# The entry into attention of a fused transformer layer: in what order the row maxima of the first two attention units are worked out

## The chip, the cores and the metric

The kernel runs on one core of a Trainium2 chip. It has five engines with a queue each: TensorE (PE in the profile, its weight loads PEld), VectorE (DVE), ScalarE (ACT), GpSimd (POOL) and SyncE (SP), which here only issues DMAs. The metric is the time of one execution in microseconds (us), as the median of several. Stretches and places below are in us from the start of the profiled execution's span.

## The reference, cut to what matters

One layer over 2048 latent tokens of width 1024, with 256 context tokens in front. What bears on the change is the gates at the end of the input projection, and the attention:

```python
p_x = h_x @ w_in[l]                      # ... q, u, vg, ga (gate_attn), gb (gate_gmlp)
k_all = jnp.concatenate([k_c, k_x], axis=2)      # 256 context + 2048 latent keys
v_all = jnp.concatenate([v_c, v_x], axis=2)
attn_x = merge_heads(attend_blocked(q_x, k_all, v_all))
...
def attend(q, k, v):
    s = jnp.einsum('bkgqd,bknd->bkgqn', q, k, preferred_element_type=jnp.float32)
    p = jax.nn.softmax(s, axis=-1).astype(v.dtype)
    return jnp.einsum('bkgqn,bknd->bkgqd', p, v)
```

There are 8 query heads of 64 columns and 2 key/value heads. A softmax needs a reference for each query, here its largest score, ahead of the exponentials.

## The kernel before

**Gates.** The projection ends with eight gate groups (`Gate`, g = 0 to 7) on a block of 1024 tokens. Each is computed with seven products in the place of eight (p in the order 0, 1, 5, 6, 4, 2, 3, the table `SUMS`), and each product is 12 matmuls of 128x512: four slices of 128 rows by three terms of a split number (lines 1742 to 1744). The last two groups, 6 and 7, run interleaved: (6,0), (7,0), (6,1), (7,1), (6,5), (7,5), and so on to (6,3), (7,3). Below, (g,p) is product p of group g. PSUM is eight banks of 128x512, in two groups of four while the projection runs (`psum({"a": 4, "b": 4})`). Group 6 holds one bank of "a" through all of its products, group 7 one of "b". Between products ScalarE moves seeds in and out of that bank and takes the tanh (line 2167), and VectorE adds sums (lines 2181 and 2186).

**Units.** Attention has 16 units (`Unit`): a block of 512 queries by two heads. `u` is the first unit and `v` the second. For each unit come, in this order:

- `load`, `cast`, `remainder`: its queries come from DRAM and are split into a high and a low half (casts on ScalarE, line 2217; remainders on VectorE, line 2223).
- `maxima(n)`: the next n of 18 items on a list. An item is a matmul for each of the two heads (four of half the width for the two context items), with 64 rows of the array each, head 0 in rows 0 to 63 and head 1 in rows 64 to 127 (line 2240), and behind them one reduction per head on VectorE over 512 columns (lines 2246 and 2251). Each item takes two banks.
- `reference`: one small reduction over all partial maxima (line 2258).
- `leading`: a transpose on PE (line 2266), a copy on ScalarE (line 2268) and eight small DMAs on SP (line 2271), which put the reference into the low half's first row.
- for each of 18 key tiles j, in three groups of six: `first` and `second`, two score matmuls each (lines 2285 and 2304; `second` reads the low half and so the reference), two exponentials on ScalarE (line 2308), later `values` (line 2316) and `gather`, the sum of the exponentials on GpSimd or VectorE (lines 2336 and 2333).

In `attend`, while unit i runs, the maxima of unit i + 1 are worked out, three at a time at two places of the first and second group. The first unit has no unit ahead of it. So the function `tail`, which the projection calls after each product of the last gates, does the first unit's maxima and the first six of the second unit's. Before: two of the first unit's behind each of nine products from (6,5) on; all that is left, `reference`, `leading` and six of the second unit's behind the last product, (7,3). Attention then opens all eight banks as one group.

**What sets the order.** The code emits instructions, and the tile framework's scheduler may reorder them on each engine, by what they wait for. Ranges in `self.fixed` keep PE and VectorE in the written order; the whole of `attend` is such a range, the end of the projection is not. Before, all maxima take banks of group "b", of which group 7 holds one: three are left for items that need two.

Of the kernel before, what the change touches and what calls it, by code (L numbers as in the profile page):

```python
# [29 lines left out]
TB = 512  # L30
# [20 lines left out]
def f32(ap):  # L51
    return ap.bitcast(F32)
# [20 lines left out]
class Kern:  # L73
# [1178 lines left out]
    def attend(self, units, late, mod):  # L1252
        self.psum({"b": 8})
        begin = self.here()
        old, pend = None, []

        def run(lo, hi):
            for j in pend[lo:hi]:
                owner.values(j)

        def ordered(work):
            at = self.here()
            work()
            self.loads.append(range(at, self.here()))

        def gather():
            for j in pend:
                owner.gather(j)

        for i, u in enumerate(units):  # L1270
            at = lambda n: units[n] if 0 <= n < len(units) else None
            nxt, far, old, older = at(i + 1), at(i + 2), at(i - 1), at(i - 2)
            for gi, g in enumerate(range(0, NKT, GROUP)):
                group = range(g, g + GROUP)
                step = nxt if gi < 2 else far
                for j in group:
                    u.first(j)
                    u.second(j)
                    if j % GROUP == 2 and far and gi == 0:
                        far.load()  # L1280
                    if j % GROUP == 4 and nxt and gi == 2:
                        ordered(nxt.leading)
                    if not nxt:
                        ordered(lambda: next(late, None))
                owner = u if gi else old
                run(0, 1)
                if step:
                    step.maxima(3)
                run(1, 4)
                if gi == 1 and far:  # L1290
                    far.cast()
                if gi == 2 and old:
                    old.sums()
                if step:
                    step.maxima(3)
                run(4, GROUP)
                if gi == 0:
                    if old:
                        old.leave()
                    u.o = self.bank([TB])  # L1300
                gather()
                if gi == 0:
                    if i:
                        next(mod, None)
                    if older:
                        older.inverse()
                if gi == 2 and far:
                    far.remainder()
                if gi == 1:
                    if nxt:  # L1310
                        nxt.reference()
                    if old:
                        old.join()
                pend = list(group)
        for _ in mod:
            pass
        owner = units[-1]
        for j in pend:
            owner.values(j)
            owner.gather(j)  # L1320
        units[-2].inverse()
        units[-1].join([self.sb("raw", [TB]) for _ in range(2)])
        self.fixed.append(range(begin, self.here()))
# [664 lines left out]
    def build(self):  # L1988
        self.constants()
        self.mod_head()  # L1990
        units = [Unit(self, b, p) for b in range(NB) for p in range(NH // 2)]
        self.KA, self.KB, self.V = ([None] * (NB + 1) for _ in range(3))
        for c in range(NB + 1):
            self.KA[c], self.KB[c] = [None] * NKV, [None] * NKV

        def key_load(kv):
            for c in range(NB + 1):
                n = TB if c else CTX
                ka = self.KA[c][kv] = self.h2([TB], F32R)
                self.nc.sync.dma_start(f32(ka[:, :n]), self.k_d[c][kv][:, :n])  # L2000

        def low_load(kv):
            for c in range(NB + 1):
                n = TB if c else CTX
                kb = self.KB[c][kv] = self.h2([TB], F32R)
                self.nc.sync.dma_start(f32(kb[HD:, :n]), self.k_d[c][kv][:HD, :n])
                self.nc.scalar.copy(kb[:HD, :n], self.lead[:HD].broadcast_to([HD, n]))

        def value_load(cs):
            for c in cs:  # L2010
                n = TT if c else CTX // P
                v = self.V[c] = self.h2([TT, P])
                src = self.rows(self.pr_d[0][c - 1][0], slice(P, 2 * P)) if c else self.vc_d[:, :n]
                self.nc.sync.dma_start(v[:, :n], src)

        def tail(g, p):
            u, v = units[0], units[1]
            n = KC - 2
            if (g, p) == (n + 1, 0):
                u.load()  # L2020
                key_load(0)
                u.cast()
                u.remainder()
            elif (g, p) == (n + 1, 1):
                low_load(0)
            elif (g, p) == (n, 5):
                u.maxima(2)
            elif g >= n and p not in (0, 1):
                if (g, p) == (n + 1, 5):
                    v.load()  # L2030
                    v.cast()
                    v.remainder()
                    value_load((0, 1))
                if (g, p) == (n + 1, 6):
                    key_load(1)
                    value_load((2, 3, 4))
                if (g, p) == (n + 1, 4):
                    low_load(1)
                u.maxima(2)
                if (g, p) == (n + 1, 3):  # L2040
                    u.maxima(len(u.todo))
                    u.reference()
                    u.leading()
                    v.maxima(6)

        self.project(tail)
        self.close("front")
        self.open("mid")
        self.open("pre", side="right")
        first = {}  # L2050
        late = self.br_inputs(0, first)
        self.g1b = self.sb("g1", [D])
        mod = self.mod_part(lambda: self.sb("raw", [TB]), ("g1",))
        self.attend(units, late, mod)
        h, w = self.operand_lists(), {0: {}}
        w1 = self.w1_ops(0, w[0], True)
        late = self.merge(first, late, units[-1], h, w1)
        self.ffn(h, w, w1, late)
        self.close("rest", "back", "pre")
        self.psum_stack.close()  # L2060
        self.order()
# [134 lines left out]
class Unit:  # L2196
# [28 lines left out]
    def maxima(self, n):  # L2225
        k, nc = self.k, self.nc
        for _ in range(n):
            if not self.todo:
                return
            c, t = self.todo.pop(0)  # L2230
            halves = ((0, slice(0, HD), k.KA), (1, slice(HD, P), k.KB))
            ps = [k.bank([TB]) for _ in range(2)]
            for s in range(2) if c == "ctx" else (0,):
                tok = slice((t + s) * P, (t + s + 1) * P)
                for h, rows, keys in halves:
                    if c == "ctx":
                        out, key = ps[h][:, s * CTX : (s + 1) * CTX], keys[0][self.kv]
                    else:
                        out, key = ps[h], keys[c][self.kv]
                    nc.tensor.matmul(  # L2240
                        out, self.qa[h][rows, tok], key[rows, : out.shape[-1]],
                        start=True, stop=True,
                    )
            for h in range(2):
                if c == "ctx":
                    nc.vector.tensor_reduce(
                        out=self.mx[:, t : t + 2, h, 0:1],
                        in_=ps[h].rearrange("p (s k) -> p s k", s=2), axis=AX.X, op=ALU.max,
                    )
                else:  # L2250
                    nc.vector.tensor_reduce(  # L2251
                        out=self.mx[:, t, h, c : c + 1], in_=ps[h], axis=AX.X, op=ALU.max
                    )
# [175 lines left out]
```

## Time and profile before

| | us |
|---|---|
| median of 3 runs (lowest, highest) | 3018.83 (3016.13, 3022.55) |
| profiled execution, its own time | 3009.05 |
| span of the profiled execution | 3007.2 |
| PE busy in the span | 2931.6 |
| DVE busy | 2062.5 |
| ACT busy | 1417.9 |
| POOL busy | 652.8 |
| maxima reductions on DVE (line 2251), 512 of them | 313.0 |
| mean granted TensorE clock | 0.994 |

The profile shows one execution. The clock is a share of full speed. The durations of PE's matmuls overlap, since a matmul starts before the one before it has ended, so how long one really takes is read from the distance of two starts. "Idle before" names, behind an arrow, what ended a wait.

### The profile page before, as it was taken

The page shows a single profiled execution, that of the slowest core. Times are in us where ns is not written, and L with a number is a line of the kernel's source. Part 1 is how long each engine was busy: PE and PEld are TensorE (multiplying, and loading weights), DVE is VectorE, ACT ScalarE, POOL GpSimd, SP SyncE. Part 2 cuts the span into 40 slices and gives each one's busy share as a digit, 9 for nine tenths or more (in the row PEclk, how much of TensorE's full clock was granted, in tenths as well). Part 3 has the DMA queues.
Part 4 walks back from the last instruction along what each step waited for, and adds up shares of the span by engine and source line. Part 5 has one row for each costly group of instructions (what it writes and reads, how often), then busy time and mean ns, then how long its engine had stood idle before and what let it go on. Part 6 is the DMA issues. An engine that isn't in the chain of part 4 may idle for free. (4 is left out here: it accounts for less than half of the span.)

```text
span 3007.2 us, 37935 instructions
## 1 busy us (share of the span) xinstructions
PE 2931.6 (97%) x13325; PEld 2206.7 (73%) x13325; DVE 2062.5 (69%) x2983; ACT 1417.9 (47%) x2318; POOL 652.8 (22%) x470
## 2 busy tenths in 40 slices
PE   7899999989999999999999989999999999999999
PEld 5778788876555555556888878888887888888887
DVE  5866487765788888867555587776676766654555
ACT  5554865553544545444222354444454344444432
POOL 0000000001999899894211200000000000000000
PEclk9999999999999999999999999999999999999999
DMA  7587866774010010016776658888766544447564
GB/s 276 184 295 272 307 215 217 256 247 140 24 36 26 25 37 22 22 36 191 238 215 194 183 198 308 307 305 303 261 219 224 186 154 154 154 154 277 210 209 155
DMA packets 386175, 559.04 MB, mean 186 GB/s; under 512 B 38640, under 2 KB 192416, under 8 KB 385984
## 3 DMA queue, kind: packets, MB, share of 16 engines
q1 hardware_dynamic: 373616, 535.89, 53.7%
q10 hardware_dynamic: 12368, 20.73, 1.8%
q8 instruction: 105, 1.72, 0.2%
q14 instruction: 86, 0.70, 0.1%
HBM read 379.75 MB, written 176.69 MB: 185 GB/s over the span
## 5 line engine op out<-in xcount | busy, mean ns | idle before, releaser
L2251 DVE TENSOR_REDUCE ts<-b 128x1 f32<-128x512 f32 x512 | 313.0, 681 | 75.3 <-PE b L2240 75.2
L2336 POOL TENSOR_TENSOR ac<-ac,p 128x512 f32<-128x512 f32 x214 | 306.3, 1463 | 50.5 <-ACT p L2308 50.5
L1858 DVE TENSOR_TENSOR b<-b,b 128x1024 fp32r<-128x1024 f32 x170 | 200.7, 1220 | 135.7 <-ACT b L1857 135.4
L1857 ACT CAST b<-b 128x1024 fp32r<-128x1024 f32 x170 | 170.6, 1050 | 222.2 <-PE b L1744 100.1
L2308 ACT ACTIVATE p<-b 128x512 f32<-128x512 f32 x384 | 194.1, 627 | 168.6 <-PE b L2304 168.1
L1743 PE MATMUL b<-b,b 128*128 128x512 f32 x680 | 265.2, 390 | 2.8 <-DVE b L1858 2.7
L1742 PE MATMUL b<-b,b 128*128 128x512 f32 x680 | 266.0, 391 | 1.6 <-DVE f L1879 1.4
L1744 PE MATMUL b<-b,b 128*128 128x512 f32 x680 | 264.7, 389 | 0.0
L2336 POOL TENSOR_TENSOR ac<-p,p 128x512 f32<-128x512 f32 x32 | 52.4, 1656 | 746.0 <-DMA raw<-in_w_mod 741.3
L2336 POOL TENSOR_TENSOR ac<-ac,t 128x512 f32<-128x512 f32 x152 | 205.0, 1378 | 0.0
L2285 PE MATMUL b<-h,h 128*128 128x512 f32 x576 | 188.0, 406 | 3.9 <-ACT p L2308 2.2
L2316 PE MATMUL b<-p,h 128*64 128x512 f32 x768 | 186.5, 609 | 0.0
L2304 PE MATMUL b<-h,h 128*128 128x512 f32 x576 | 179.1, 392 | 0.0
L1743 PE MATMUL b<-hb,b 128*128 128x512 f32 x446 | 173.8, 390 | 0.0
L1752 DVE TENSOR_TENSOR f<-f,b 128x512 f32<-128x512 f32 x160 | 109.0, 682 | 78.6 <-issue 45.8
L1742 PE MATMUL b<-hb,b 128*128 128x512 f32 x415 | 162.0, 390 | 0.3 <-DVE f L1752 0.3
L1744 PE MATMUL b<-hb,b 128*128 128x512 f32 x415 | 161.3, 389 | 0.0
L2285 PEld LDWEIGHTS b<-h,h 128*128 128x128 f32 x576 | 104.1, 189 | 65.1 <-DVE ts L2251 26.0
L1743 PEld LDWEIGHTS b<-b,b 128*128 128x128 f32 x680 | 127.6, 188 | 31.4 <-DVE b L1858 4.7
L1742 PEld LDWEIGHTS b<-b,b 128*128 128x128 f32 x680 | 127.6, 188 | 29.5 <-ACT b L1857 2.3
L1744 PEld LDWEIGHTS b<-b,b 128*128 128x128 f32 x680 | 127.7, 188 | 26.4
L157 POOL TENSOR_TENSOR bw<-bw,bw 128x512 fp32r<-128x512 f32 x58 | 75.8, 1328 | 235.7 <-ACT bw L153 235.7
(436 smaller groups left out, 7207.0 us busy)
## 6 DMA issues: line engine op xcount, KB each, us to landing
ao_d<-f SPq DMA_DIRECT2D x224, 256.0 KB
f<-in_w_ff SPq DMA_DIRECT2D x48, 1024.0 KB
b<-ao_d SPq DMA_DIRECT2D x85, 512.0 KB
b<-w2o_d SPq DMA_DIRECT2D x85, 512.0 KB
w2o_d<-f SPq DMA_DIRECT2D x112, 256.0 KB
f<-in_w_in SPq DMA_DIRECT2D x38, 512.0 KB
f<-x_d SPq DMA_DIRECT2D x64, 256.0 KB
hb<-ao_d SPq DMA_DIRECT2D x54, 256.0 KB
```

The lines of the kernel that those rows point to most:

```text
L1742: mm(ps, wh, hh, start=start and k == 0, stop=False, skip_group_check=True)
L1743: mm(ps, wh, hl, start=False, stop=False, skip_group_check=True)
L1744: mm(ps, wl, hh, start=False, stop=k == len(w) - 1, skip_group_check=True)
L1752: nc.vector.tensor_tensor(out=out, in0=in0, in1=in1, op=op)
L1857: nc.scalar.copy(h, f32(l))
L1858: nc.vector.tensor_tensor(out=l, in0=f32(l), in1=f32(h), op=ALU.subtract)
L2251: nc.vector.tensor_reduce(out=self.mx[:, t, h, c : c + 1], in_=ps[h], axis=AX.X, op=ALU.max)
L2285: self.nc.tensor.matmul(self.pts[j][h], k.KA[c][self.kv][:, ks], self.qa[h], start=True, stop=False, skip_group_check=True,)
L2304: self.nc.tensor.matmul(s, k.KB[c][self.kv][:, ks], self.qb[h], start=False, stop=True, skip_group_check=True,)
L2308: self.nc.scalar.activation(pt[h], s, AF.Exp)
L2316: nc.tensor.matmul(self.o[h * HD : (h + 1) * HD, :], k.V[c][:, i, self.kv * HD : (self.kv + 1) * HD], pt[h], start=j == 0, stop=j == NKT - 1,)
L2336: nc.gpsimd.tensor_tensor(out=self.acc[e][:, h], in0=old[:, h], in1=pt[h], op=ALU.add)
```

## The change

The maxima take a bank of each group ("a" for head 0, "b" for head 1) as long as there are two groups. `tail` does three of the first unit's behind each of the six products (6,5), (7,5), (6,6), (7,6), (6,4), (7,4), then `reference`, `leading` behind (6,2), and two of the second unit's behind (6,2), (7,2) and (6,3). From (6,5) on, the order of PE and VectorE is as written. In `attend`, the first unit's first group does the second unit's next six maxima three behind its third key tile and three behind its sixth, in place of both threes at the group's end.

```diff
@@ attend
                     if j % GROUP == 2 and far and gi == 0:
                         far.load()
+                    if not i and j in (2, 5):
+                        step.maxima(3)
...
                 run(0, 1)
-                if step:
+                if step and (i or gi):
                     step.maxima(3)
                 run(1, 4)
...
-                if step:
+                if step and (i or gi):
                     step.maxima(3)
@@ tail, n = 6
-            elif (g, p) == (n, 5):
-                u.maxima(2)
             elif g >= n and p not in (0, 1):
+                if (g, p) == (n, 5):
+                    begin.append(self.here())
...
-                u.maxima(2)
-                if (g, p) == (n + 1, 3):
-                    u.maxima(len(u.todo))
+                if (g, p) == (n, 2):
+                    u.leading()
+                if p in (2, 3):
+                    v.maxima(2 if g == n or p == 2 else 0)
+                else:
+                    u.maxima(3)
+                if (g, p) == (n + 1, 4):
                     u.reference()
-                    u.leading()
-                    v.maxima(6)
-
+
+        begin = []
         self.project(tail)
+        self.fixed.append(range(*begin, self.here()))
@@ Unit.maxima
-            ps = [k.bank([TB]) for _ in range(2)]
+            ps = [k.bank([TB], tag=tag) for tag in (("a", "b") if "a" in k.banks else "bb")]
```

Line numbers move by six behind `tail`: 2240 becomes 2246, 2285 becomes 2291, and so on.

Three places show what this does to the order. First PE around the start of product (6,4). Names: `a_6539` is group 6's bank, `b_6583` group 7's; the target of a maxima matmul is its bank, `h_66..` with the lower numbers are keys, `h_6614` and `h_6615` the two heads' queries. Before:

```order
L1744 MATMUL b_6583<-h_4070,f_1179_6580 128x512
L2240 MATMUL b_6839<-h_6606,h_6614 128x512
L2240 MATMUL b_6840<-h_6688,h_6615 128x512
L2240 MATMUL b_6845<-h_6608,h_6614 128x512
L1742 MATMUL a_6539<-h_4104,f_1166_6489 128x512
L1743 MATMUL a_6539<-h_4105,f_1166_6489 128x512
L2240 MATMUL b_6846<-h_6691,h_6615 128x512
L1744 MATMUL a_6539<-h_4104,f_1167_6490 128x512
L1742 MATMUL a_6539<-h_4109,f_1166_6489 128x512
```

The same place after the change:

```order
L1746 MATMUL b_6583<-h_4070,f_1179_6580 128x512
L2246 MATMUL a_6857<-h_6612,h_6614 128x512
L2246 MATMUL b_6858<-h_6697,h_6615 128x512
L2246 MATMUL a_6863<-h_6606,h_6614 128x512
L2246 MATMUL b_6864<-h_6688,h_6615 128x512
L2246 MATMUL a_6869<-h_6608,h_6614 128x512
L2246 MATMUL b_6870<-h_6691,h_6615 128x512
L1744 MATMUL a_6539<-h_4104,f_1166_6489 128x512
L1745 MATMUL a_6539<-h_4105,f_1166_6489 128x512
```

The fourth matmul of a round stood inside the product, where a bank came free; now six stand in one piece between two products.

Second, PE where the first unit's reference is transposed (`ident` and `ts` on the transpose's row). Before, behind the last product (7,3), with eight more maxima matmuls and then the first score product behind these rows:

```order
L1744 MATMUL b_6583<-hx_4229,t_1177_6576 128x512
L2266 MATMUL b_7018<-ident,ts_7016 8x128
L2240 MATMUL b_7030<-h_6604,h_6752 128x256
L2240 MATMUL b_7031<-h_6685,h_6753 128x256
L2240 MATMUL b_7030<-h_6604,h_6752 128x256
L2240 MATMUL b_7031<-h_6685,h_6753 128x256
L2240 MATMUL b_7038<-h_6604,h_6752 128x256 x2
L2240 MATMUL b_7039<-h_6685,h_6753 128x256 x2
```

After the change it stands behind (6,2):

```order
L1746 MATMUL a_6539<-hx_4184,e_1225_6790 128x512
L2272 MATMUL b_6974<-ident,ts_6956 8x128
L2246 MATMUL a_6986<-h_6604,h_6758 128x256
L2246 MATMUL b_6987<-h_6685,h_6759 128x256
L2246 MATMUL a_6986<-h_6604,h_6758 128x256
L2246 MATMUL b_6987<-h_6685,h_6759 128x256
L2246 MATMUL a_6994<-h_6604,h_6758 128x256
L2246 MATMUL b_6995<-h_6685,h_6759 128x256
L2246 MATMUL a_6994<-h_6604,h_6758 128x256
L2246 MATMUL b_6995<-h_6685,h_6759 128x256
L1744 MATMUL b_6583<-hx_4169,t_1232_6824 128x512
```

Product (7,2) follows two of the second unit's maxima, and no maxima stand between the last product and the first score. On ScalarE at the same place (`m_6596` from `b_6583` is the last gate's tanh, `h_7259` and `h_7260` are the third unit's queries, `p_1283` the first exponentials). Before:

```order
L2167 ACTIVATE m_6552<-a_6539 128x512
L2167 ACTIVATE m_6596<-b_6583 128x512
L2268 COPY t_1267_7020<-b_7018 8x128
L2217 CAST h_7259<-t_1290_7109 128x512
L2308 ACTIVATE p_1283_7086<-b_7082 128x512
L2308 ACTIVATE p_1283_7086<-b_7083 128x512
```

And after the change:

```order
L2173 ACTIVATE m_6552<-a_6539 128x512
L2223 CAST h_7259<-t_1290_7109 128x512
L2173 ACTIVATE m_6596<-b_6583 128x512
L2223 CAST h_7260<-t_1291_7110 128x512
L2314 ACTIVATE p_1283_7086<-b_7082 128x512
L2314 ACTIVATE p_1283_7086<-b_7083 128x512
```

The copy of the reference has moved up, ahead of five gate instructions, and the second cast, which stood twelve exponentials later, now stands ahead of the first one. `b_7082`, the first score bank, is the one that `b_6583` held.

Third, PE in attention's first group, after the change, from the third key tile's last score product on:

```order
L2310 MATMUL b_7101<-h_6620,h_6688 128x512
L2246 MATMUL b_7115<-h_6606,h_6758 128x512
L2246 MATMUL b_7116<-h_6688,h_6759 128x512
L2246 MATMUL b_7121<-h_6608,h_6758 128x512
L2246 MATMUL b_7122<-h_6691,h_6759 128x512
L2246 MATMUL b_7127<-h_6610,h_6758 128x512
L2246 MATMUL b_7128<-h_6694,h_6759 128x512
L2291 MATMUL b_7133<-h_6614,h_6606 128x512
```

Six maxima matmuls now part the third from the fourth key tile; six more stand behind the sixth, where all twelve stood before.

## The prediction

> **What bounds the kernel now.** First the page's head, for who is busy.
>
> ```profile
> span 3007.2 us, 37935 instructions
> PE 2931.6 (97%) x13325; PEld 2206.7 (73%) x13325; DVE 2062.5 (69%) x2983; ACT 1417.9 (47%) x2318; POOL 652.8 (22%) x470
> ```
>
> TensorE (PE) is busy in 97% of the span, so what it waits or works longer at one place moves all that follows. Then the table by stretches, cut at PE's own milestones at the entry into attention (columns: stretch, its length, then busy time and count for PE, PEld, DVE, ACT, POOL, then granted clock, DMA share, GB/s).
>
> ```profile
> 692.36:731.03 38.67, 38.67 (x149) 23.67 (x149) 26.82 (x44) 10.43 (x19) 0.00 (x0) 1.00 0.46 134
> 731.03:738.49 7.46, 5.77 (x19) 2.50 (x17) 6.72 (x12) 0.73 (x2) 0.00 (x0) 0.78 0.12 38
> 736.00:738.49 2.49, 1.49 (x4) 0.57 (x3) 2.49 (x6) 0.00 (x0) 0.00 (x0) 0.50 0.02 1
> 738.49:742.07 3.58, 3.58 (x8) 2.81 (x9) 0.54 (x1) 1.79 (x4) 0.00 (x0) 0.50 0.76 217
> 738.49:749.52 11.03, 10.56 (x37) 7.04 (x37) 3.68 (x7) 7.21 (x14) 6.96 (x6) 0.84 0.47 143
> 749.52:756.07 6.55, 6.22 (x25) 4.35 (x25) 4.13 (x7) 4.85 (x10) 4.97 (x5) 1.00 0.00 0
> 782.33:795.39 13.06, 13.06 (x62) 6.86 (x61) 11.48 (x15) 7.48 (x16) 9.22 (x8) 1.00 0.10 31
> ```
>
> Four things stand here. From 692.36 to 731.03 the last nine gate products run with the first unit's maxima between them. From 731.03 to 738.49 PE only does the second unit's first six maxima, and there VectorE (DVE) is busy for 6.72 of 7.46: it is the bound. The clock falls to 0.50 there and stays so until 742.07, eight matmuls into attention. In the settled attention (last row) PE is busy for all of 13.06, and the others are not; so what the entry saves is carried through attention, and behind it by the 97%.
>
> **The prices**, from PE's timeline (start, duration, engine, line, operation, count).
>
> ```profile
> 686.92 0.39 PE L1742 MATMUL b<-h,f 128*128 128x512 f32 x1
> 689.64 0.39 PE L1742 MATMUL a<-h,t 128*128 128x512 f32 x1
> 692.45 0.73 PE L2240 MATMUL b<-h,h 64*128 64x256 f32 x6
> 705.58 0.73 PE L2240 MATMUL b<-h,h 64*128 64x512 f32 x3
> 706.24 0.50 PE L1742 MATMUL a<-h,f 128*128 128x512 f32 x1
> 706.90 0.49 PE L2240 MATMUL b<-h,h 64*128 64x512 f32 x1
> 707.32 0.50 PE L1744 MATMUL a<-h,f 128*128 128x512 f32 x1
> 709.82 0.73 PE L2240 MATMUL b<-h,h 64*128 64x512 f32 x3
> 757.08 0.96 PE L2240 MATMUL b<-h,h 64*128 64x512 f32 x6
> 757.97 2.79 PE L2316 MATMUL b<-p,h 128*64 128x512 f32 x12
> ```
>
> A gate product of 12 matmuls takes 689.64 - 686.92 = 2.72 us. With two maxima (four matmuls, split three and one) a round is 709.82 - 705.58 = 4.24, so two maxima cost 1.52. Three maxima in one piece are six matmuls in 757.97 - 757.08 = 0.89; with about 0.2 for going over to them and back I take 1.09 (a change of operand shape costs: the lone matmul at 706.90 holds the next gate matmul until 707.32). So three in a row cost less than two in the split.
>
> ```profile
> 692.99 2.49 DVE L2246 TENSOR_REDUCE ts<-b 128x2 f32<-128x512 f32 x4 [4.67 <-PE b L2240]
> 699.04 1.28 DVE L2223 TENSOR_TENSOR h<-t,h 128x512 fp32r<-128x512 f32 x2
> 710.00 0.69 DVE L2181 TENSOR_TENSOR m<-m,a 128x512 f32<-128x512 f32 x1 [1.41 <-PE a L1744]
> 734.17 4.86 DVE L2251 TENSOR_REDUCE ts<-b 128x1 f32<-128x512 f32 x8
> 746.39 7.26 DVE L2251 TENSOR_REDUCE ts<-b 128x1 f32<-128x512 f32 x12 [7.35 <-PE b L2240]
> ```
>
> A reduce costs DVE 7.26 / 12 = 0.605 and each maxima needs two; a 128x512 sum or remainder about the same. Three maxima are 3.63 of DVE against 2.72 + 1.09 = 3.81 of PE: nearly even, and the sums decide.
>
> **The change, part by part.**
>
> (1) The first unit's 18 maxima, now six blocks of three. DVE's first reduce began at 692.99 and does so again. Up to the reference it has 36 reduces (21.8) and six others (two query remainders, two weight remainders, the sums of products (6,4) and (7,4): 3.6). I add 0.9 for the remainders, which wait in their fixed place for casts behind product (7,5), 0.8 for five handovers and 0.2 for the reference itself: 692.99 + 27.3 = 720.3. PE's own work to that point is six blocks and six products, 692.45 + 6.5 + 16.3 = 715.3. So DVE is the bound and PE waits some 5 us, in pieces: for its second and third pair of banks in each block and for the reference in front of the transpose. Bounds: 718.6 (DVE never waits: 692.99 + 21.8 + 3.6 + 0.2) and 722.7 (each block pays a second change of shape, 6 x 0.4). I take 720.3, nearer to the rows of before, where DVE takes up a result 0.54 after its matmul began (746.39 behind PE's 745.85, quoted below).
>
> (2) The second unit's six maxima, two each behind (6,2), (7,2), (6,3). Four reduces are 2.42 and a sum 0.6, against 2.72 + 0.85 of PE, so PE is the bound: transpose 0.2, three blocks 0.8 to 0.85, three products 2.72 give 10.9 and 731.2. The 7.46 of DVE-paced work at the end are gone.
>
> (3) The first score product now waits for the last gate's tanh, since both use that bank. Before, that tanh was long over.
>
> ```profile
> 731.03 0.27 PE L2266 MATMUL b<-ident,ts 128*8 128x128 f32 x1
> 731.94 5.55 PE L2240 MATMUL b<-h,h 64*128 64x256 f32 x12 [0.20 <-ACT m L2167]
> 731.29 0.60 ACT L2167 ACTIVATE m<-b 128x512 f32<-128x512 f32 x1 [3.65 <-PE b L1744]
> 738.49 1.22 PE L2285 MATMUL b<-h,h 128*128 128x512 f32 x2 [1.00 <-DVE ts L2251]
> ```
>
> The tanh ends at 731.89, 0.9 after PE was free. So the first score comes at 731.2 + 0.9 = 732.1 in place of 738.49: **6.4 us earlier**, or 4.0 to 8.1 by the bounds of (1).
>
> (4) The reference row (transpose, copy, eight 0.5 KB DMAs) moves from behind all gate products to ahead of the last three. On SP's queue it passes the last four gate stores, one of which comes to stand between its second and third DMA. On ScalarE (ACT) its copy goes ahead of the seed copies and tanhs of the last three products, and on DVE the reference ahead of the sum of (6,2): all of these wait for the reference at 720.3, and the first of them, the seed for (6,3), is not wanted before 724.
>
> ```profile
> 732.32 5.04 SPq L2271 DMA_DIRECT2D h<-t  x8
> 737.40 1.87 SPq L2212 DMA_DIRECT2D t<-q_d  x3
> 740.07 0.62 ACT L2217 CAST h<-t 128x512 fp32r<-128x512 f32 x1 [8.05 <-DMA t<-q_d]
> ```
>
> Issuing takes 5.04 and it was there by 739.5, at most 2.2 after the last issue. From a copy at 721.1, with one store between, the last issue ends near 726.6, landed by 728.8: 3 us ahead of need. I cost it at nothing; cover gone, it costs one for one.
>
> (5) Attention's first group: the maxima come behind the third and sixth key tile, three each, in place of six at the end. Two gains: the clock, if PE no longer starves before it, gives back 8 matmuls in 3.58 against 8 x 2.72 / 12 = 1.81: 1.8. And the 12 maxima matmuls, which took 3.67 (next rows) where settled attention takes 2 x 0.89, lie beside the exponentials.
>
> ```profile
> 745.85 3.57 PE L2240 MATMUL b<-h,h 64*128 64x512 f32 x12
> 749.52 1.10 PE L2285 MATMUL b<-h,h 128*128 128x512 f32 x2
> ```
>
> Of those 1.9 I expect 1.5, in the two groups together; DVE still needs 7.26 for the 12 reduces, and banks come free at that pace. Bounds of (5): 1.1 (the clock alone, less 0.7 where scores wait behind maxima for a bank) and 3.7 (both in full); I take 3.2.
>
> **Sum**: 6.4 + 3.2 = 9.6 us. The profiled execution took 3009.05 (span 3007.2 and 1.85 around it), so 2999.4 there. The median of the runs is 3018.83, 9.8 above it; the same saving gives **3009.2**. 0.2% is 6.0 us, about what a measurement of this kernel can tell from no change.
>
> **The clock, weighed.** The rows have 0.50 from 736.00 on, although PE still did a matmul for each freed bank, 0.6 us apart. The Trainium skill, page "TensorE: Matmul & The Clock Gate", Part 1, says that the clock goes to half after an idle window of about 3.4 us and comes back after as long a busy one. By that rule no wait here is long enough, since an estimated wait is under 2 us, and the sum stays 9.6 us; read by the rows, thin work is enough to lose it, which is the third rival below. The return at 742.07, 3.58 after the scores began, agrees with the page.
>
> **The rivals.**
>
> A: DVE's pace eats more. Where PE gets its banks one at a time, the two halves of a pair go apart, and each block pays a lone matmul as at 706.90 (0.4). Six blocks, plus a sum at its fixed place in DVE's order that holds the reduces behind it, make 4 to 5 us: 3013.9. For it: DVE is busy or handing over in all of the 27.3 us, so nothing there can be made up. Against it: a late reduce costs PE only at the third pair.
>
> B: the wait goes over to ScalarE. Both casts of the third unit's queries now stand ahead of the first exponential, and the second one needs a load that SP issues behind the store of (6,3). By the rows: product (6,3) ends at 727.6, its tanh at 728.5, its store at 729.0, the load's issue at 729.5; landing 2.1 to 2.7 after issue (as at 740.07) and a cast of 0.6 give 732.2 to 732.8, with the first exponential wanted at 733.0. A landing later by 4 us stops PE when its eight banks are full, nearly one for one: 3013. That the change would not do what it says is the near relation of this: the 7.46 gap only renamed. Against that stands the new order, in which no maxima are left between the last product and the first score.
>
> C, on the other side: **the clock falls in the blocks**. If the thin stretches (a pair per 1.2 us) in front of each product count as idle, as they did at 731.94 to 736, a product runs at half speed, 2.7 us more. Six times that is 16.3, less 9.6: slower by 6.7, 3025.5. It decides from about four falls (10.9 against 9.6). Against it: before the fall PE had been thin for some 4 us from 731.94, here for at most 2.4 between dense products of 2.72.
>
> **Chances**: forecast 0.68, A 0.20, B 0.08, C 0.04. The forecast alone spans 3007.0 (8.1 + 3.7) to 3013.7 (4.0 + 1.1) by the bounds of (1) and (5); A and B reach 3014, and the runs scatter by 3 either way, so the range is 3003.5 to 3016.0, leaving out C and the edge of the others. Faster by over 0.2% (under 3012.8): nearly all of the forecast, and a little of A and B, 0.70. Within 0.2%: A, B and the forecast's upper edge, 0.26. Slower: 0.04.
>
> **What would show it.** The transpose near 720 and the first score near 732; clock 1.00 all the way from 692 to 760; DVE with hardly a gap from 699 to 720 and PE's waits there on reduces; the first values product near 746.5 instead of 756.07; the distance from unit to unit unchanged behind it. Wrong: a transpose after 723 (A), an exponential that waits on a query load (B), a clock below 1 in a block (C), or a unit distance that grows, which would say that attention isn't bound by PE.

## The result and the profile after

The median of 22 runs is 3013.27 us (3008.52 to 3020.84), beside 3019.69 us for 22 runs of the kernel before on the same chip: a ratio of 0.9979, 95% interval 0.9973 to 0.9986, or 6.4 us less. The same kernel timed twice more, each time beside the kernel before, gave 0.9972 (0.9957 to 0.9986) and 0.9986 (0.9977 to 0.9994). So the three series put the gain at 0.14 to 0.28%. One execution of a kernel of the experiments (`pool_gap`) took 4640.74 us at a granted clock of 0.58, and that kernel's ratio leaves it out.

The profiled execution took 3012.09, in fact 3 us more than the one of before. Its page:

```profile
span 3010.1 us, 37936 instructions
PE 2931.4 (97%) x13325; PEld 2210.1 (73%) x13325; DVE 2069.9 (69%) x2983; ACT 1418.8 (47%) x2318; POOL 650.8 (22%) x470
```

The two spans can't be compared as they stand: this execution reached PE's first maxima matmul at 696.22, that of before at 692.45, and other executions at 692.3 to 704.1, on the same instructions. So from here on, places are counted from that matmul. PE's milestones after the change, from its timeline:

```profile
723.29 0.27 PE L2272 MATMUL b<-ident,ts 128*8 128x128 f32 x1 [0.97 <-DVE ts L2264]
735.15 0.73 PE L2291 MATMUL b<-h,h 128*128 128x512 f32 x2 [0.75 <-ACT m L2173]
749.62 1.08 PE L2322 MATMUL b<-p,h 128*64 128x512 f32 x4
765.38 0.37 PE L2272 MATMUL b<-ident,ts 128*8 128x128 f32 x1 [3.54 <-DVE ts L2264]
```

The transpose comes 27.07 behind the first maxima matmul (before 38.58), the first score 38.93 (before 46.04), the first values product 53.40 (before 63.62). Up to there **10.2 us are saved**, in every place that the prediction named. But the last row, the transpose for unit 1, has a wait of 3.54 that was not there before. By stretches (columns as before):

```profile
696.22:723.29 27.07, 25.70 (x114) 17.18 (x113) 25.57 (x44) 7.63 (x14) 0.00 (x0) 1.00 0.55 162
723.29:735.15 11.86, 11.11 (x54) 7.74 (x54) 8.59 (x14) 4.34 (x8) 0.00 (x0) 1.00 0.31 99
735.15:749.62 14.47, 13.83 (x60) 9.74 (x60) 7.36 (x12) 11.26 (x23) 10.44 (x9) 1.00 0.33 102
749.62:765.38 15.76, 12.22 (x58) 6.13 (x58) 14.06 (x14) 4.53 (x10) 14.42 (x12) 0.96 0.00 0
765.38:771.00 5.62, 5.62 (x21) 2.74 (x23) 0.88 (x2) 2.97 (x7) 5.04 (x5) 0.50 0.02 3
771.00:807.15 36.15, 36.15 (x166) 19.08 (x167) 31.96 (x44) 17.17 (x35) 26.46 (x20) 1.00 0.11 34
```

Row four is 15.76 long; before, the same stretch (756.07 to 768.14) took 12.07. In row five the clock is 0.50, so unit 1 takes 807.15 - 765.38 = 41.77 in place of 39.30. Together 3.69 + 2.47 = 6.2 us are given back there. The timeline of all engines at that place:

```profile
756.58 2.53 POOL L2342 TENSOR_TENSOR ac<-ac,t 128x512 f32<-128x512 f32 x2
...
758.38 6.75 DVE L2339 TENSOR_TENSOR ac<-p,t 128x1024 f32<-128x1024 f32 x1
...
759.06 4.99 POOL L2342 TENSOR_TENSOR ac<-ac,p 128x512 f32<-128x512 f32 x4
...
765.05 0.18 DVE L2264 TENSOR_REDUCE ts<-ts 128x8 f32<-128x40 f32 x1
765.22 1.08 ACT L2314 ACTIVATE p<-b 128x512 f32<-128x512 f32 x2 [4.10 <-DVE ac L2339]
```

VectorE's sum of exponentials (key tiles 2 and 4), which took 1.21 before the change, takes 6.75. GpSimd (POOL) adds exponentials at the same time, one instruction behind the other, until 764.05; VectorE's sum ends 1.1 later, about its own duration. The reference for unit 1 stands behind that sum in VectorE's fixed order, and the transpose waits for the reference. An exponential also waited, 4.10, for the sum.

Before the change, that sum began while GpSimd stood still (VectorE's timeline, then GpSimd's, which is idle from 764.06 to 765.26):

```profile
764.83 1.21 DVE L2333 TENSOR_TENSOR ac<-p,t 128x1024 f32<-128x1024 f32 x1
...
759.10 4.96 POOL L2336 TENSOR_TENSOR ac<-ac,t 128x512 f32<-128x512 f32 x4
765.26 8.12 POOL L2336 TENSOR_TENSOR ac<-ac,p 128x512 f32<-128x512 f32 x6 [1.20 <-ACT p L2308]
```

In the second profile of the very same kernel (`again`) the sum also begins while GpSimd adds without a gap, but it gets in at the next boundary between two adds:

```profile
755.38 1.79 DVE L2339 TENSOR_TENSOR ac<-p,t 128x1024 f32<-128x1024 f32 x1
757.09 0.18 DVE L2264 TENSOR_REDUCE ts<-ts 128x8 f32<-128x40 f32 x1
...
753.55 2.53 POOL L2342 TENSOR_TENSOR ac<-ac,t 128x512 f32<-128x512 f32 x2
756.03 6.02 POOL L2342 TENSOR_TENSOR ac<-ac,p 128x512 f32<-128x512 f32 x4
```

Here it is GpSimd that waits: its four adds take 6.02 in place of 4.99. So the two engines exclude each other in these instructions, and which one comes first at a boundary differs from one execution to the next. The Trainium skill, page "SBUF — State Buffer", section "Who interferes with whom", states this: an instruction of VectorE with two inputs in SBUF contends with one of GpSimd that reads SBUF, and the ports that the two share are an exclusive lock. The traces agree, and show that the loser can lose at four boundaries in a row: the add under way when the sum began and the next three each handed over to another add.

### The profile page after: what moved, and what is told of

Read it like the earlier page. It is cut to its first block, busy times and chain, and to the rows that moved or that the text cites. A ratio compares the mean times of both kernels' runs of the same rounds, so it can differ in the third digit from the quotient of the medians.

```text
span 3010.1 us, 37936 instructions
## 1 busy us (share of the span) xinstructions
PE 2931.4 (97%) x13325; PEld 2210.1 (73%) x13325; DVE 2069.9 (69%) x2983; ACT 1418.8 (47%) x2318; POOL 650.8 (22%) x470
## 4 chain that ended last, share of the span: by engine, by line
PE 82%; DMA 6%; DVE 6%; ACT 3%; issue 2%; SPq 1%; ACTq 0%; POOL 0%; DVEq 0%; POOLq 0%
PE b L1744 14%; PE b L1745 14%; PE b L1746 14%; PE b L2322 8%; PE b L2291 4%; PE b L2310 4%; PE b L186 4%; PE b L187 4%; PE b L188 4%; PE b L2246 3%; PE a L1744 2%; PE a L1746 2%; PE a L1745 2%; PE b L192 1%; DMA m<-ws_d 1%
## 5 line engine op out<-in xcount | busy, mean ns | idle before, releaser
L2257 DVE TENSOR_REDUCE ts<-b 128x1 f32<-128x512 f32 x492 | 302.0, 681 | 69.7 <-PE b L2246 69.7
```

Source lines behind the costliest of these rows:

```text
L2257: nc.vector.tensor_reduce(out=self.mx[:, t, h, c : c + 1], in_=ps[h], axis=AX.X, op=ALU.max)
```

## The experiments

All places are in us behind PE's first maxima matmul, from PE's timeline in each kernel's one profile. "Sum" is the duration of VectorE's first sum of exponentials. `threes_last`, `attend_alone`, `free_gates` and `one_group` were run once each (3004.30, 3012.65, 3003.55 and 3025.03 us); as the stretch ahead of the first maxima matmul alone varies by 12 us, their places say more than their times.

| kernel | transpose, unit 0 | first score | first values product | transpose, unit 1 | last unit's transpose | sum |
|---|---|---|---|---|---|---|
| before | 38.58 | 46.04 | 63.62 | 75.69 | 639.09 | 1.21 |
| after | 27.07 | 38.93 | 53.41 | 69.16 | 637.19 | 6.75 |
| again | 27.91 | 39.77 | 54.29 | 66.34 | 629.73 | 1.79 |
| again2 | 27.07 | 38.94 | 53.39 | 65.45 | 628.84 | 1.84 |
| pool_gap | 27.07 | 38.93 | 53.45 | 65.50 | 629.69 | 1.21 |
| pool_gap2 | 27.07 | 38.96 | 53.41 | 65.47 | 629.66 | 1.22 |
| sum_later | 27.92 | 39.82 | 54.27 | 66.32 | 629.72 | 2.08 |
| ref_first | 27.92 | 39.82 | 54.34 | 66.39 | 629.79 | 1.57 |
| threes_last | 27.08 | 38.95 | 56.01 | 68.07 | 631.46 | 1.22 |
| attend_alone | 38.58 | 46.04 | 61.53 | 77.43 | 642.39 | 6.89 |
| free_gates | 33.33 | 43.12 | 57.65 | 69.71 | 633.10 | 1.79 |
| one_group | 44.11 | 59.34 | 73.86 | 85.91 | 649.31 | 1.79 |
| spread | 27.79 | 36.04 | 51.85 | 63.91 | 627.30 | 1.26 |
| spread_load | 27.80 | 36.03 | 51.54 | 63.60 | 627.79 | 1.22 |

The first question was whether the collision belongs to the new order or to one execution.

**again**, the changed kernel, unedited.

> The changed kernel once more, nothing edited. In its first profile VectorE's first sum of exponentials in unit 0 (ac<-p,t) began at 758.38 and lasted 6.75 us in place of 1.21, the second unit's transpose waited 3.54 us for it, and the clock then fell. Theory L (lock): VectorE's sum cannot start while GpSimd's sums follow each other without a gap, and in this order they always do so at that place; so the sum lasts 5 us or more again, the distance from the first values product of unit 0 to the transpose of unit 1 is 15.8 again (before: 12.1), and the ratio to before is 0.998. Theory R (chance): the two engines only happened to collide in that one execution; the sum lasts under 2.5 us here and the distance is about 12.1.

The sum took 1.79, the stretch to unit 1's transpose 12.05, the ratio was 0.9972. Theory R holds for this execution: the saving up to the last unit's transpose is 639.09 - 629.73 = 9.4.

**pool_gap** makes a gap in GpSimd's run; the line chooses the key tiles that VectorE sums, in unit 0 alone.

```diff
-        e = j in (LAST_ON_VECTOR if self.last else ON_VECTOR)
+        e = j in (LAST_ON_VECTOR if self.last else ON_VECTOR if self.b or self.p else (2, 4, 8, 10, 14))
```

> Unit 0 alone: the sum over key tile 10 goes from GpSimd to VectorE, where it comes 19 us later than the sum in question. GpSimd then has nothing to do from about 756.6 until the exponentials of tile 12 at 758.7, so there is a gap when VectorE's sum (tiles 2 and 4) begins, at its old place at 758.4 behind the twelve reduces. L: the sum lasts about 1.2 to 2.3, the transpose of unit 1 no longer waits (12.1 behind the first values product), the clock stays at 1.00, and the time falls by 3.7 + 2.5 = 6 us against the changed kernel: ratio to before 0.996. Rival D (data): the sum is long for a reason of its own (what it reads comes late, or its memory is busy); then it lasts 6 us again and the ratio stays at 0.998.

GpSimd stood still ahead of the sum, and its next six adds, which overlap the sum, take 8.12 as they do before the change, where six with nothing beside them take 7.48 (`after`, from 746.67) (VectorE's timeline, then GpSimd's):

```profile
756.40 1.21 DVE L2339 TENSOR_TENSOR ac<-p,t 128x1024 f32<-128x1024 f32 x1
...
752.11 2.52 POOL L2342 TENSOR_TENSOR ac<-ac,t 128x512 f32<-128x512 f32 x2
756.84 8.12 POOL L2342 TENSOR_TENSOR ac<-ac,p 128x512 f32<-128x512 f32 x6 [2.21 <-ACT p L2314]
```

The sum took 1.21 as expected of L, but since `again` doesn't lose the contest either, this one profile proves nothing about the cause. The ratio was 0.9977 (0.9966 to 0.9988), not 0.996, and that of the changed kernel in the same series 0.9972: no 6 us were there to be won in that series. Rival D is settled by the profiles where the sum was held: each time it ended 1.07 to 1.08 behind the end of GpSimd's run of adds (765.13 behind 764.05 above; 771.09 behind 770.01 in `attend_alone`; 1185.70 behind 1184.63 in a later unit of the changed kernel), so GpSimd held it, and not its data. The sum over tile 10 costs something too: unit 1 takes 40.07 in place of 39.30.

**sum_later** takes the sum away from that place.

```diff
+        e = j in (LAST_ON_VECTOR if self.last else ON_VECTOR if self.b or self.p else (8, 10, 14))
```

> Unit 0 alone: VectorE sums key tiles 8, 10 and 14 in place of 2, 4, 8 and 14, so that its first sum comes behind group 2 and the reference of unit 1 follows the twelve reduces directly. GpSimd has two more half sums by then. L: the reference comes at about 758.4, the transpose of unit 1 does not wait, clock 1.00, ratio to before 0.996. Rival V (VectorE is late by its reduces alone): the transpose waits as before, 0.998. Rival P (GpSimd falls behind with the sums it takes over, 5 us by the end of the first group, and its buffers hold up the exponentials): 0.998 or worse, with waits of ScalarE on GpSimd's ac.

No wait at the transpose, as in `again`; ratio 0.9971 (0.9962 to 0.9980). Rivals V and P are out: the transpose doesn't wait for the reduces, and the units keep their 39.30 and 40.16. It doesn't speak for L either, since `again` has no wait with the sum in place.

**ref_first** puts the reference ahead of the sum.

```diff
+                if gi == 1 and nxt and not i:
+                    nxt.reference()
                 gather()
...
-                    if nxt:
+                    if nxt and i:
                         nxt.reference()
```

> Unit 0 alone: the reference of unit 1 stands ahead of VectorE's sum of tiles 2 and 4 in place of behind it; GpSimd is left as it is. L: the sum is still held for 5 us, and with it the buffer of tile 2 for which an exponential waited 4.10 us in the changed kernel's profile. So the transpose itself comes without a wait, but PE's next score products then wait for banks: most of the loss stays, ratio 0.9975 (1 us gained, 3 at most). Rival T: the transpose's wait was all; then all 6 us come back, 0.996.

The sum was not held in this execution (1.57), so L and T can't be told apart by it; the ratio was 0.9972 (0.9961 to 0.9984). Whether the exponential's wait of 4.10 alone would cost PE as much stays open.

**again2 and pool_gap2** time both kernels once more, in one series.

> The changed kernel a third time. So far VectorE's first sum in unit 0 met GpSimd's run of sums in all executions of this order of maxima (changed kernel, again, ref_first, free_gates, attend_alone); it got in at the first boundary between two of GpSimd's instructions in three (1.6 to 1.8 us) and waited for the run's end in two (6.75 and 6.89). Theory R (chance): either outcome, nothing between; the first values product to the transpose of unit 1 is 12.1 or 15.8. The clock within the blocks of the first unit's maxima: either 1.00 throughout (transpose at 27.1 behind the first maxima matmul) or half for some 3.5 us behind the third block (27.9).

> The kernel with a gap in GpSimd's run at that place (tile 10 of unit 0 summed on VectorE), timed a second time beside the changed kernel. If about half of the changed kernel's executions lose 6 us to the contest, this one's median lies up to 3 us under that of the changed kernel in the same call; if the contest is rare, they agree within 1 us. In the profile the first sum lasts under 1.5 us in any case.

The changed kernel: 3010.39 (ratio 0.9986); with the gap: 3006.17 (ratio 0.9974, 0.9965 to 0.9983). That is 4 us, more than the 3 that a loss of 6 in half the executions was expected to give, and the two intervals overlap. The first series had it the other way round (3004.14 and 3006.24), so the times don't settle how often the contest is lost. The profiles count it: seven executions had GpSimd's run at that place (`after`, `again`, `again2`, `ref_first`, `free_gates`, `one_group`, `attend_alone`), and the sum lost in **two of the seven** (6.75 and 6.89). In the others it took 1.6 to 1.8. Of the changed kernel itself it is one in three. Where the sum begins doesn't tell the two cases apart: in `again2` it began 62.15 behind the first maxima matmul, with 0.76 of GpSimd's add left, in the first profile at 62.16, with 0.73 left.

The second question was what each part of the change is worth.

**threes_last** undoes part (5).

```diff
-                    if not i and j in (2, 5):
-                        step.maxima(3)
...
-                if step and (i or gi):
+                if step:
                     step.maxima(3)
```

> Part (5) undone, all else as in the changed kernel: in unit 0's first group both threes stand at the group's end again. Places are counted from PE's first maxima matmul (changed kernel, second profile: first score product 39.8, first values product 54.3, so 14.5 apart; before 46.0 and 63.6, so 17.6 apart). As predicted (1.8 from the clock, the rest from the place of the maxima): the first score stays at 39.8, the clock stays at 1.00, and the first values product comes 17.6 - 1.8 = 15.8 behind it, 1.3 later than in the changed kernel. Rival (the place of the maxima is all of part (5), the clock falls here too): 17.6. Rival (the clock is all): 14.5.

The first score is at 38.95 and the first values product 17.06 behind it, near the first rival's 17.6. The clock fell here although PE came into the scores from dense work at full clock (PE's timeline, then a row of the table by stretches):

```profile
739.84 0.73 PE L2244 MATMUL b<-h,h 64*128 64x512 f32 x4
741.12 2.29 PE L2244 MATMUL b<-h,h 64*128 64x512 f32 x8 [0.55 <-DVE ts L2255]
743.50 1.14 PE L2289 MATMUL b<-h,h 128*128 128x512 f32 x2
744.44 1.05 PE L2308 MATMUL b<-h,h 128*128 128x512 f32 x2
```
```profile
743.50:747.96 4.46, 4.35 (x10) 2.93 (x11) 4.14 (x7) 2.04 (x4) 3.16 (x3) 0.62 0.00 0
```

The last eight of twelve maxima matmuls wait for VectorE's reductions, most of them in pairs 0.6 apart, and the score pairs behind them take 1.05 in place of 0.62. So the place of the maxima is worth 17.06 - 14.47 = 2.6 of the 3.1, and the better entry only 0.5. This kernel shows a second thing. Its sum meets a gap, as it did before the change:

```profile
760.00 1.22 DVE L2337 TENSOR_TENSOR ac<-p,t 128x1024 f32<-128x1024 f32 x1
...
760.43 8.12 POOL L2340 TENSOR_TENSOR ac<-ac,p 128x512 f32<-128x512 f32 x6 [2.17 <-ACT p L2312]
```

With the maxima at the group's end, the next exponentials come late and GpSimd runs dry just then. **Part (5) closes this gap**, and that is what exposes the sum.

**attend_alone** is the kernel before with part (5) (the edit of threes_last the other way round).

> The kernel before with part (5) alone. The first score stays at 46.0 behind the first maxima matmul. As predicted: the clock is still at half when the scores begin, since VectorE paces PE ahead of them, and the first values product follows 17.6 - 1.3 = 16.3 later, at 62.3. Rival (the place of the maxima is worth nothing by itself): 17.6, 63.6.

The first values product came at 61.53, 15.5 behind the first score: 2.1 gained, more than predicted; and with the maxima in their new places the denser entry is worth 15.5 - 14.5 = 1.0. And the sum lost its contest, without any change to the gates, so it is part (5) that exposes it:

```profile
764.20 6.89 DVE L2335 TENSOR_TENSOR ac<-p,t 128x1024 f32<-128x1024 f32 x1
...
765.03 4.98 POOL L2338 TENSOR_TENSOR ac<-ac,p 128x512 f32<-128x512 f32 x4
```

Unit 1's transpose is 77.43, later than before the change (75.69), and unit 1 takes 40.84 in place of 39.30: the loss ate more than part (5) had won, and the last unit's transpose is 3.3 later than before the change.

**free_gates** leaves the order at the end of the gates to the scheduler.

```diff
-        self.fixed.append(range(*begin, self.here()))
```

> The changed kernel without the fixed order over the end of the gates: the scheduler then lets the third pair of a block slip into the next product, one matmul at a time, so that PE need not wait for VectorE in front of a product. If VectorE bounds this stretch, as the prediction has it, the transpose stays within 0.7 of 27.9 behind the first maxima matmul and the first score within 0.7 of 39.8: the fixed order is worth nothing here. Rival (lone matmuls cost PE 0.4 each, two in each of four blocks): 3.2 later, transpose at 31. Rival (PE's waits in front of the products were the loss): up to 3 earlier.

Both forecasts of "within 0.7" failed: the transpose came 6.3 and the first score (43.12) 4.2 later than in the changed kernel's first profile, and PE is never idle up to the transpose (33.33 busy of 33.33). Two rounds of a product and a block, by the first maxima matmul of each, here and in the changed kernel:

```profile
706.83 0.49 PE L2245 MATMUL a<-h,h 64*128 64x512 f32 x1
...
707.83 0.40 PE L1745 MATMUL a<-h,f 128*128 128x512 f32 x1
708.16 0.49 PE L2245 MATMUL a<-h,h 64*128 64x512 f32 x1
708.58 0.50 PE L1746 MATMUL a<-h,f 128*128 128x512 f32 x1
...
711.72 0.49 PE L2245 MATMUL a<-h,h 64*128 64x512 f32 x1
...
716.61 0.50 PE L2245 MATMUL a<-h,h 64*128 64x512 f32 x1
```
```profile
709.68 0.49 PE L2246 MATMUL a<-h,h 64*128 64x512 f32 x1
...
713.86 0.49 PE L2246 MATMUL a<-h,h 64*128 64x512 f32 x1
...
718.06 0.49 PE L2246 MATMUL a<-h,h 64*128 64x512 f32 x1
```

4.89 against 4.18 to 4.20. The third pair's two matmuls stand alone inside the product (one of them at 708.16), and each costs PE 0.35 more than where it waits its turn in a block. So the lone matmuls of rival A are real; the fixed order keeps them out, and is worth 4 us at the first score.

**one_group** gives both banks of an item from group b again.

```diff
-            ps = [k.bank([TB], tag=tag) for tag in (("a", "b") if "a" in k.banks else "bb")]
+            ps = [k.bank([TB], tag=tag) for tag in "bb"]
```

> The changed kernel with both banks of every item from group b, as before the change: three banks are free there, so a block of six matmuls must wait for three reductions of its own before the next product can start, and VectorE then has at most three reductions (1.8 us) left to do beside a product of 2.72 + 0.3. Per block some 1.3 us of VectorE are lost: the transpose comes at 27.1 + 6 x 1.3 = 35 behind the first maxima matmul, the first score at 47, later than before the change (46.0): the second bank group is what the new order rests on. Rival (VectorE's total sets the transpose whatever the banks): transpose at 28, first score at 40.

```profile
696.13:740.24 44.11, 37.82 (x113) 23.78 (x113) 25.88 (x43) 7.72 (x14) 0.00 (x0) 0.81 0.35 99
```

The transpose comes at 44.1, 9 later than expected: the lost time of VectorE is there (25.88 busy of 44.11), and the mean clock is 0.81, which the expectation had not put into the sum. The second bank group is worth 17 us to the new order up to the transpose, and 20 up to the first score.

**spread** follows from the bound.

```diff
-                    if not i and j in (2, 5):
-                        step.maxima(3)
+                    if not i and j in (1, 3, 5):
+                        step.maxima(2 if j == 1 else 3)
...
-                if (g, p) == (n, 2):
+                if (g, p) == (n + 1, 2):
                     u.leading()
-                if p in (2, 3):
-                    v.maxima(2 if g == n or p == 2 else 0)
-                else:
-                    u.maxima(3)
-                if (g, p) == (n + 1, 4):
+                if (g, p) in ((n + 1, 2), (n, 3)):
+                    v.maxima(2)
+                elif p != 3:
+                    u.maxima(2 if (g, p) in ((n + 1, 5), (n, 6), (n, 4)) else 3)
+                if (g, p) == (n, 2):
                     u.reference()
```

> A version meant to be faster than both. If VectorE bounds the stretch up to the transpose (PE waits there for about 5 us in pieces), then the first unit's 18 maxima can lie behind seven products (3, 2, 2, 3, 2, 3, 3) and the transpose behind the eighth, at about 28 as now but with two more products done by then; four of the second unit's maxima stay behind (7,2) and (6,3), and two more move into unit 0's first group (2, 3 and 3 behind its tiles 1, 3 and 5). Then the first score comes at 28.1 + 0.3 + 0.8 + 2.7 + 0.8 + 2.7 + 0.9 = 36.3 behind the first maxima matmul in place of 39.8, with up to 0.6 of a wait for the reference row; the first group gives 0.8 back. Sum: 2 to 3 us faster than the changed kernel, ratio to before 0.996. Rival (PE, not VectorE, sets the transpose): the transpose comes at 31, the first score at 39, no gain.

The transpose stays at 27.79 with one more product ahead of it (not two, as I had counted), so VectorE sets it; the first score comes at 36.04. The first group then takes 15.8 in place of 14.5, and 2.4 us of the 3.7 are left (627.30 against 629.73). That is against `again`; against `again2`, whose clock didn't fall in the blocks, the first score is 2.9 earlier and 1.5 are left. The ratio is 0.9962 (0.9949 to 0.9976): with spread_load the fastest order of the study, though its interval overlaps the changed kernel's.

**spread_load** adds pool_gap's line and an earlier load of the third unit's queries.

```diff
+                if (g, p) == (n, 2):
+                    units[2].load()
...
-                    if j % GROUP == 2 and far and gi == 0:
+                    if j % GROUP == 2 and far and gi == 0 and i:
                         far.load()
```

> The spread version with the gap in GpSimd's run, and with the third unit's queries loaded ahead of the first unit's reference row (in spread, ScalarE's cast of them waited 2.71 us for the load and the first exponential began at 735.36, 3.2 behind the first score product, in place of 1.1 in again). If that wait is what costs spread 15.8 from the first score to the first values product in place of 14.5, then the first values product comes at 50.5 behind the first maxima matmul (spread 51.9, again 54.3), and the ratio to before is 0.9957. Rival (the eight maxima of unit 0's first group cost it): 51.9, 0.9962.

The exponentials now begin 1.0 behind the first score, yet the first values product comes at 51.54 and the ratio is 0.9968 (0.9956 to 0.9980): 0.3 of the expected 1.4. What is left is most likely the rival, the eight maxima: `spread`'s own expectation had 0.8 for the two that moved in, and PE has short waits behind the first two of their blocks:

```profile
734.22 0.73 PE L2248 MATMUL b<-h,h 64*128 64x512 f32 x4
735.50 0.73 PE L2293 MATMUL b<-h,h 128*128 128x512 f32 x2 [0.55 <-DVE ts L2259]
...
737.54 0.97 PE L2248 MATMUL b<-h,h 64*128 64x512 f32 x6
738.81 0.73 PE L2293 MATMUL b<-h,h 128*128 128x512 f32 x2 [0.31 <-DVE ts L2259]
```

At the last unit's transpose this kernel is 0.5 behind `spread` (627.79 against 627.30), since the line from `pool_gap` makes unit 1 take 40.07 here too.

## Why the prediction was right, and where not

The direction and the mechanism at the entry were right: 9.6 us forecast, and 9.4 (`again`) and 10.2 (`again2`) saved up to the last unit's transpose where the sum of unit 0 is not held. The time was less good: 3009.2 forecast, 3013.27 measured, which is inside the range of 3003.5 to 3016.0, and 6.4 saved beside the kernel before. That is 0.21%, with an interval of 0.14 to 0.27%, so that it came out faster by just over 0.2% and not just under is luck. Step by step:

- **(1), the blocks.** Forecast 720.3, which is 27.85 behind the first maxima matmul; measured 27.07. VectorE is the bound (25.57 busy of 27.07, and `spread`). The 0.8 for five handovers was the error: VectorE's reductions follow each other without a gap from 702.58 on; the 0.9 for the remainders' casts was there (a wait of 0.94).
- **(2) and (3).** Forecast 10.9 + 0.9 = 11.8 from the transpose to the first score, measured 11.86, of which 0.75 is the wait for the tanh.
- **(4), the leading row.** Forecast for its last issue 726.6, which is 34.15; measured 730.53 - 696.22 = 34.3. It cost nothing.
- **(5), the first group.** Forecast 3.2, measured 17.58 - 14.47 = 3.1. (The terms in its text, 1.8 and 1.5, add up to 3.3.) The split was wrong: I gave 1.8 to a clock that was to stay up through the denser entry and 1.5 to the place of the maxima. `threes_last` shows that the twelve maxima at the group's end bring the clock down by themselves.
- **C, the clock in the blocks.** It happens, but at most once in an execution's blocks, not six times: in three of the eight profiles that share this tail (`again`, `sum_later`, `ref_first`) the clock fell behind the third block, and the transpose came 0.84 later (27.9). From `again`:

```profile
700.00:704.00 4.00, 3.62 (x12) 1.88 (x12) 4.00 (x7) 0.59 (x1) 0.00 (x0) 0.98 0.15 58
704.00:706.00 2.00, 2.00 (x6) 1.54 (x5) 2.00 (x5) 0.00 (x0) 0.00 (x0) 0.50 0.62 171
706.00:708.00 2.00, 2.00 (x10) 1.15 (x8) 1.24 (x3) 0.51 (x2) 0.00 (x0) 0.69 0.92 245
```

  The third block is thin because VectorE has two query remainders to do first: PE's last four maxima matmuls stand 0.6 apart. So of the two readings that the prediction weighed, the one by the rows held, that thin work is enough to lose the clock. The Trainium skill, page "TensorE: Matmul & The Clock Gate", Part 1, says that the window by which the gate judges runs freely; that the same code falls in three of eight executions agrees.
- **A and B.** A's lone matmuls cost 0.35 each in `free_gates` and are absent from the fixed order. B's wait of a cast for its load appeared in `spread`, 2.71, and cost about 0.3 by `spread_load`.
- **The step that failed** is the last one, "the distance from unit to unit unchanged behind it". It was so in `again` (39.30), not in the changed kernel's first profile (41.77, and 3.69 ahead of it). A unit distance that grows was one of the prediction's signs of being wrong. It carried the saving on because in settled attention PE is busy for all of 13.06 "and the others are not"; it has no term for the sums of exponentials in unit 0, so a wait of VectorE for GpSimd stood at nothing, and the runs showed 3.69 and 2.47 for it where the sum is held. The change moved VectorE's first sum out of a gap of GpSimd's into the middle of its run.

The accounts close. Against `again2`, the changed kernel's first profile gave back 3.71 + 2.47 = 6.18 in units 0 and 1, and 2.17 more in a later unit, where another sum was held for 5.27 and the unit took 42.36 in place of 40.19: 637.19 - 6.18 - 2.17 = 628.84, which is what `again2` has. If two in seven lose 6.2 us and three in eight 0.84, the mean saving is 10.25 - 1.8 - 0.3, about 8; the three measured ratios stand for 8.4, 6.3 and 4.2 (1 less the ratio, times the median of the kernel before). This last step is an estimate from few profiles, and how often the contest is lost is not settled. Much of the scatter lies in stretches that the change doesn't touch: up to the first maxima matmul the profiles have 692.3 to 704.1, from the last unit's transpose to the end 1674.6 to 1683.8. Of the changed kernel's three profiles, `again2` saved the most up to that transpose and took 3010.87; `again` took 3000.82.

## What to carry to other kernels

When a change makes one engine's work come earlier, look at what the engines that share something with it are doing at the new moment; a place that was free of contest only because something else was late may not stay so. Two profiles of one kernel can differ by more than the change is worth (7.5 us here, 637.19 against 629.73), so a wait that one of them shows is looked for in a second before anything is built on it. And a block of work that another engine paces belongs between dense pieces, a few instructions at a time and in one piece, not as lone instructions within them.

## What the runs showed of the hardware

- VectorE's sum with both inputs in SBUF, if it begins while GpSimd runs adds without a gap, mostly gets in at the next boundary between two of them, but not always. In the 14 profiles of this study 287 sums of exponentials up to the last unit began during an add that the next one followed within 0.1. Of these, 284 took 1.2 to 2.3 and ended 1.08 to 1.13 behind the end of that add; three took 5.27, 6.75 and 6.89 and ended 1.07 to 1.08 behind the end of GpSimd's whole run.
- The clock went to half while PE still did a matmul, or a pair, every 0.6 us: behind twelve maxima matmuls paced by VectorE (`threes_last`, 3.66 from 739.84 to 743.50), and in three of eight executions behind the third block (2.8 from 700.04 to 702.85 in `again`).
- A single matmul of 64 rows between matmuls of 128 rows costs PE about 0.35 more than in a block of six (4.89 against 4.19 for a round with two such).
